# The last half-step of a two-layer decoder trunk: a different inverse root, store queue, place of the norm's weights and number of idle matmuls

## The chip, the cores and the metric

The kernel runs on one core of one Trainium2 chip. The metric is the device time of one execution in microseconds; times given for a kernel are medians over several runs. A profile is one execution taken with the hardware profiler. Its span goes from the first to the last instruction of the program.

The engines are called PE or TensorE (matmul), DVE or VectorE, ACT or ScalarE, POOL or GpSimd, and SP or SyncE (here only issuing DMA transfers). ACT, too, issues some of the transfers, in order with its arithmetic.

## What is computed

The input is 512 tokens of 1024 values. One layer with a convolution module and one with stick-breaking attention each hold two half-step feed-forward blocks. The change lies in the last of the four blocks and in the norm that ends the computation:

```
def rms_norm(x, g):
    xf = x.astype(jnp.float32)
    y = xf * lax.rsqrt(jnp.mean(xf * xf, axis=-1, keepdims=True) + RMS_EPS)
    return (y * g.astype(jnp.float32)).astype(x.dtype)

def swiglu_ffn(x, w_gate, w_up, w_down):
    return (jax.nn.silu(x @ w_gate) * (x @ w_up)) @ w_down

    # at the end of reference(), for the last layer:
    h = h + HALF_STEP * swiglu_ffn(rms_norm(h, ffn2_norm[layer]), ...)
    return rms_norm(h, final_norm)
```

## The kernel before

**Layout.** All is kept transposed: eight chunks of 128 channels (`d` = 0 to 7) on the partitions, 512 tokens along the free dimension. `res[d]` holds the running sum, in the tile `xpar`, which holds the input and the parameters too. Each fp32 product is made of three matmuls of high and low parts (`mm3`, lines 365 to 367). The channel of a norm's weight is a partition, so the weight is a per-partition scale (`col("final", d)`); the inverse root differs by token, so it has to be laid out as a row that is equal on all partitions.

**Order of the work.** The feed-forward blocks are planned: `planned` (line 461) adds steps with estimated costs, and `Plan.issue` writes them out in an order found from these costs. Only the last part, `tail` (line 1479), is written out by hand for PE, VectorE, ScalarE and GpSimd: the lines 1571 to 1611 are the order on each of these four engines. SP is not among them. The plan covers the output chunks 0 to 4 of the last third; `tail` takes the chunks 5, 6 and 7 (`a`, `b`, `e`) and works on two halves of 256 tokens (`h` = 0 and 1), so that the first half's norm and stores run while the second half's products are made.

**The parts of `tail`.** `product(d, h)` makes the matmuls into `pe`. `leave(d, h)` adds half of that to `res` on VectorE (line 1496) and squares the sum on ScalarE (line 1500). `add` (line 1503) adds the squares up in `acc_out`. `sums(h)` sums over the partitions: eight small matmuls against a column of 1/1024 (line 397), the last four from the squares of chunk 7 directly. The result `ss` has the 256 tokens as 128 partitions by 2.

`root(h)` makes the inverse root of these 2 columns. `inv_root` (lines 403 to 410) takes a first guess from the bits of the number and does three Newton steps of three instructions each; with the addition of epsilon (line 1520) these are 12 dependent instructions on VectorE. The result is split in a high and a low part (lines 1523 and 1524).

`diagonal_rows(h)` multiplies the identity by these columns, one block on VectorE (line 1535) and one on ScalarE (line 1533) for each part, and `row(h)` (line 1542) multiplies a matrix of ones by them, which gives the row of factors on all partitions, twice: `pb_out..v` for VectorE, and `pb_out..a`, which `rows(h)` copies to SBUF for GpSimd (line 1561).

The output of a chunk is made in one of two ways. Either `gain(d, h)` has multiplied by the weight on ScalarE earlier (line 1546), and `scale(d, h)` multiplies by the row on GpSimd (line 1551); that is so for the chunks 5, 6, 7 of the first half and 5, 6 of the second. Or `scale` does both at once on VectorE (line 1554). It then issues the store of 128 KB at once (line 1557): on SP for odd chunks, on ScalarE's queue for even ones. A store on ScalarE's queue waits there, in order, until its data is made.

`idle()` (line 1567) issues 16 matmuls whose result nobody reads, between the last sums and the last row. `STEADY` is their number.

## Time and profile before

| | us |
|---|---|
| median of 3 runs | 1886.19 |
| lowest and highest of them | 1885.01, 1886.81 |
| the profiled execution's own time | 1885.87 |
| its span | 1884.1 |
| PE busy | 1863.1 (99% of the span) |
| VectorE busy | 1495.5 (79%) |
| ScalarE busy | 996.1 (53%) |
| GpSimd busy | 219.4 (12%) |

Busy PE time counts matmuls that overlap in the pipeline, so 99% does not say that PE works at its peak. Times in the timeline count from the start of the span. In the chain of waits, each piece is the work or wait that the next piece was released by, followed back from the last instruction. In the rows of a timeline stand the start, the length, the engine, the line, the operation, output and inputs, and, in brackets, how long the engine had been idle before and what ended that. The queue of an engine that issues a DMA is written with a q (ACTq, SPq).

### The profile page before, as it was taken

The numbers are of one execution on the slowest core, as the hardware profiler recorded it, in microseconds if no ns is written. First come the engines' busy times: TensorE is split into PE (matmuls) and PEld (weight loads), VectorE is DVE, ScalarE is ACT, GpSimd is POOL, SyncE is SP. The second block draws the span as 40 slices with busy tenths as digits, with TensorE's granted clock in tenths as the row PEclk, the third lists the DMA queues.
The fourth block names the chain that finished last, engine by engine and source line by source line (L and its number), as shares of the span: only waits on it lengthen the run. The fifth ranks groups of instructions, "written<-read, shape, count | busy, mean of one in ns | idle before, by whom it ended". The sixth has DMA issues, their size and how long they took to land.

```text
span 1884.1 us, 29763 instructions
## 1 busy us (share of the span) xinstructions
PE 1863.1 (99%) x11558; PEld 1676.5 (89%) x11560; DVE 1495.5 (79%) x2494; ACT 996.1 (53%) x1670; POOL 219.4 (12%) x240
## 2 busy tenths in 40 slices
PE   9999999999999999999999999999999999999998
PEld 7889989878998999898898999988888779899897
DVE  8968868689789669677995976978999689678595
ACT  5535535696655446345452544646777655345253
POOL 0000000079700000000000000004454100000000
PEclk9999999999999999999999999999999999999999
DMA  5565666644413322323252332352322132323232
GB/s 183 173 218 202 246 211 232 239 147 172 140 57 101 112 90 90 134 69 122 84 173 79 112 113 90 125 163 83 90 76 88 51 104 87 130 73 124 79 111 78
DMA packets 74269, 238.04 MB, mean 126 GB/s; under 512 B 8464, under 2 KB 11152, under 8 KB 74128
## 3 DMA queue, kind: packets, MB, share of 16 engines
q1 hardware_dynamic: 65776, 209.41, 33.6%
q10 hardware_dynamic: 8352, 26.74, 3.7%
q8 instruction: 90, 1.47, 0.3%
q14 instruction: 51, 0.42, 0.1%
HBM read 200.46 MB, written 31.46 MB: 123 GB/s over the span
## 4 chain that ended last, share of the span: by engine, by line
PE 87%; DVE 6%; DMA 3%; ACT 2%; issue 1%; POOL 0%; DVEq 0%; ACTq 0%; SPq 0%; POOLq 0%
PE bank L365 12%; PE bank L366 12%; PE bank L367 12%; PE bank L661 11%; PE bank L663 11%; PE bank L662 11%; DMA raw<-in_gu_dram 2%; PE z L1383 2%; DVE pc L1071 1%; PE pa L365 1%; PE pa L366 1%; PE pa L367 1%; PE po L367 1%; PE po L365 1%; PE po L366 1%
## 5 line engine op out<-in xcount | busy, mean ns | idle before, releaser
L459 ACT CAST high<-raw 128x1024 fp32r<-128x1024 f32 (+1 forms) x199 | 202.6, 1018 | 277.0 <-PE bank L366 220.1
L366 PE MATMUL bank<-hlo,high 128*128 128x512 f32 x686 | 267.0, 389 | 0.0
L365 PE MATMUL bank<-hhi,high 128*128 128x512 f32 x686 | 267.0, 389 | 0.0
L367 PE MATMUL bank<-hhi,low 128*128 128x512 f32 x686 | 266.9, 389 | 0.0
L460 DVE TENSOR_TENSOR low<-raw,high 128x1024 fp32r<-128x1024 f32 (+1 forms) x199 | 234.3, 1178 | 16.1 <-ACT high L459 15.7
L781 DVE SCALAR_TENSOR_TENSOR xpar<-bank,xpar 128x512 f32<-128x512 f32 x93 | 64.2, 691 | 153.3 <-PE bank L367 153.0
L661 PE MATMUL bank<-thi,wh 128*128 128x256 f32 x544 | 154.6, 284 | 1.0 <-ACT u L707 0.6
L661 PE MATMUL bank<-thi,sh 128*128 128x256 f32 x544 | 154.2, 283 | 0.3 <-ACT bank L699 0.3
L662 PE MATMUL bank<-xlo_f,high 128*128 128x256 f32 x544 | 153.9, 283 | 0.0
L663 PE MATMUL bank<-xhi_f,low 128*128 128x256 f32 x544 | 153.9, 283 | 0.0
L662 PE MATMUL bank<-tlo,sh 128*128 128x256 f32 x544 | 153.9, 283 | 0.0
L663 PE MATMUL bank<-thi,sl 128*128 128x256 f32 x544 | 153.9, 283 | 0.0
L663 PE MATMUL bank<-thi,wl 128*128 128x256 f32 x544 | 153.9, 283 | 0.0
L662 PE MATMUL bank<-tlo,wh 128*128 128x256 f32 x544 | 153.9, 283 | 0.0
L661 PE MATMUL bank<-xhi_f,high 128*128 128x256 f32 x544 | 153.9, 283 | 0.0
L367 PEld LDWEIGHTS bank<-hhi,low 128*128 128x128 f32 x686 | 128.8, 188 | 26.9
L365 PEld LDWEIGHTS bank<-hhi,high 128*128 128x128 f32 x686 | 128.8, 188 | 26.3
L366 PEld LDWEIGHTS bank<-hlo,high 128*128 128x128 f32 x686 | 128.8, 188 | 26.0
L365 PE MATMUL bank<-xhi_f,high 128*128 128x512 f32 x320 | 126.2, 394 | 0.6 <-ACT high L258 0.6
L367 PE MATMUL bank<-xhi_f,low 128*128 128x512 f32 x320 | 125.4, 392 | 0.0
L366 PE MATMUL bank<-xlo_f,high 128*128 128x512 f32 x320 | 125.4, 392 | 0.0
L460 DVE TENSOR_TENSOR sl<-st,sh 128x1024 fp32r<-128x1024 f32 x68 | 82.9, 1219 | 41.1 <-ACT sh L459 41.1
(362 smaller groups left out, 5296.4 us busy)
## 6 DMA issues: line engine op xcount, KB each, us to landing
raw<-in_gu_dram SPq DMA_DIRECT2D x174, 512.0 KB, 3.4
raw<-in_dna_dram SPq DMA_DIRECT2D x64, 512.0 KB, 3.5
plo<-in_pw_dram SPq DMA_DIRECT2D x24, 512.0 KB, 4.2
aparth<-phi ACTq DMA_DIRECT2D x24, 512.0 KB, 3.6
apartl<-plo ACTq DMA_DIRECT2D x24, 512.0 KB, 3.9
raw<-in_dnb_dram SPq DMA_DIRECT2D x32, 384.0 KB, 3.3
high<-aparth SPq DMA_DIRECT2D x21, 512.0 KB, 3.3
low<-apartl SPq DMA_DIRECT2D x21, 512.0 KB, 4.2
```

Of the source, the lines that this page charges most:

```text
L365: PE.matmul(ps, w[0], x[0], start=first, stop=False)
L366: PE.matmul(ps, w[0], x[1], start=False, stop=False)
L367: PE.matmul(ps, w[1], x[0], start=False, stop=last)
L459: plan.add("A", a, lambda: A.copy(sub(hi()), sub(src())), r=[src], w=[hi], rank=rank)
L460: plan.add("V", v, lambda: V.tensor_sub(sub(lo()), sub(src()), sub(hi()).bitcast(F32)), r=[src, hi], w=[lo], rank=rank)
L661: PE.matmul(d, a[0], b[0], start=start and q == 0, stop=False, skip_group_check=True)
L662: PE.matmul(d, a[0], b[1], start=False, stop=False, skip_group_check=True)
L663: PE.matmul(d, a[1], b[0], start=False, stop=last_, skip_group_check=True)
L781: add("V", 0.62, lambda d=d, pd=pd: V.scalar_tensor_tensor(res[d], pd(), 0.5, res[d], op0=ALU.mult, op1=ALU.add), r=[pd], w=[("res", d)], ...
L1071: add("V", 0.66 * f + 0.06 * half, lambda x=x, q=q: V.scalar_tensor_tensor(pc(), x(), q, pc(), op0=ALU.mult, op1=ALU.add), r=[gl], w=[pc], ...
L1383: PE.matmul(dst, st, m[:, a:b], start=False, stop=True, skip_group_check=True)
```

## The change

Four things are changed, all in `tail`:

- `root` takes a square root on ScalarE (with epsilon as its bias, from a new tile), then on VectorE the reciprocal and one Newton step; the table that the square root needs is loaded on ScalarE by an instruction of its own behind the first square of `tail`.
- The first half's stores are all issued on SP; the second half's stay on SP and ScalarE by turns.
- Of the second half, the chunks 0 to 4 too get the norm's weight on ScalarE. These five are placed ahead of the first half's diagonals, and those of the chunks 5 and 6, which stood behind the second root, now stand behind `rows(0)`. VectorE then only multiplies by the row for the chunks 0 to 4; chunk 7 of the second half is done as before. A new argument of `scale` says which chunks go to GpSimd; they are the same as before.
- `STEADY` is 8 instead of 16.

```
-STEADY = 16
+STEADY = 8
...
         def root(h):
             y, v = (fp.tile([P, 2], F32, name=f"{x}_out{h}") for x in ("y", "v"))
-            V.tensor_scalar_add(v, ss[h], RMS_EPS)
-            inv_root(y, v, f"out{h}", fp)
+            t = fp.tile([P, 2], F32, name=f"t_out{h}")
+            A.activation(y, ss[h], AF.Sqrt, bias=eps)
+            V.tensor_scalar(v, ss[h], -0.5, -0.5 * RMS_EPS, op0=ALU.mult, op1=ALU.add)
+            V.reciprocal(y, y)
+            V.tensor_mul(t, y, y)
+            V.tensor_mul(t, v, t)
+            V.scalar_tensor_tensor(y, t, 1.5, y, op0=ALU.add, op1=ALU.mult)
...
-        def scale(d, h):
+        def scale(d, h, on_pool=False):
             sl = TOKENS[h]
             if (d, h) in o:
-                G.tensor_mul(o[d, h], o[d, h], rs[h])
+                if on_pool:
+                    G.tensor_mul(o[d, h], o[d, h], rs[h])
+                else:
+                    V.tensor_mul(o[d, h], o[d, h], pb[h, "v"])
...
-            (nc.sync if d % 2 else nc.scalar).dma_start(out[:, d, sl], o[d, h])
+            (nc.sync if d % 2 or h == 0 else nc.scalar).dma_start(out[:, d, sl], o[d, h])
...
+        eps = fp.tile([P, 1], F32, name="eps_out")
         a, b, e = ds
...
+            V.memset(eps, RMS_EPS)
             product(a, 0)
             leave(a, 0)
+            A.preload_act_table_set("sqrt_and_others")
             add(a, 0)
...
             for d in (5, 6, 7):
                 gain(d, 0)
+            for d in range(5):
+                gain(d, 1)
             diagonal_rows(0)
...
             rows(0)
+            for d in (5, 6):
+                gain(d, 1)
             for d in (0, 5):
-                scale(d, 0)
+                scale(d, 0, d > 4)
...
             root(1)
-            for d in (5, 6):
-                gain(d, 1)
             diagonal_rows(1)
             row(1)
             rows(1)
             for d in (0, 5, 1, 2, 6, 3, 4, 7):
-                scale(d, 1)
+                scale(d, 1, d in (5, 6))
```

## The prediction

> **What bounds the kernel now.** First the head of the page, for the scale, then the chain of waits over the last 12 us, since every edit lies there.

> ```profile
> span 1884.1 us, 29763 instructions
> ```
> ```profile
> 1872.25 0.42 DVE xpar L1496
> 1872.67 0.79 DVE out L1554 x2
> 1873.46 0.43 ACT sqe L1500
> ...
> 1874.57 3.50 PE pw_out L1567 x16
> ...
> 1878.35 0.48 DVE out L1554
> ```

> The chain's columns are start, length, and what ran. The last product leaves PSUM at 1872.25, its square follows at 1873.46 and the first scaled output at 1878.35. Two pieces are not what they seem. The two DVE scalings between 1872.67 and 1873.46 read nothing that the square needs, and the 3.50 us of idle matmuls stand for a wait that runs beside them on VectorE: the root. Next the ACT queue ahead of that square, and the first and last small step of the root, from the timeline:

> ```profile
> 1873.07 0.34 ACTq L1557 DMA_DIRECT2D out_dram<-out  x1
> 1873.46 0.42 ACT L1500 ACTIVATE sqe<-xpar 128x256 f32<-128x256 f32 x1 [1.92 <-DVE out L1554]
> 1873.93 0.64 PE L397 MATMUL ss_out<-onesD,sqe 128*128 128x1 f32 x4 [1.38 <-ACT sqe L1500]
> 1874.61 0.16 DVE L1520 TENSOR_SCALAR v_out<-ss_out 128x2 f32<-128x2 f32 x1 [0.77 <-PE ss_out L397]
> 1876.97 0.17 DVE L1523 CAST dp_out<-y_out 128x2 fp32r<-128x2 f32 x1
> ```
> ```profile
> 1871.62 2.10 POOL L1551 TENSOR_TENSOR out<-out,rs_out 128x256 f32<-128x256 f32 x3 [374.87 <-ACT rs_out L1561]
> ```

> The input of the square is there at 1872.67, but ACT holds a store of an earlier half that it may only issue when GpSimd's second product (1871.62 + 2 x 0.70 = 1873.02) is done: 1873.07, 0.34 long, then the square. TensorE stood idle for 1.38 us when the last sums began at 1873.93. The root lasts from 1874.61 to 1876.97: 2.36 us, 12 dependent steps of 0.197 us.

> Last, stretches of the end, with granted clock, DMA share and GB/s in the last three columns:

> ```profile
> 1874.40:1877.70 3.30, 3.30 (x17) 3.30 (x17) 2.64 (x16) 1.43 (x4) 0.00 (x0) 0.50 0.48 170
> 1877.80:1881.10 3.30, 0.75 (x6) 0.54 (x5) 2.44 (x6) 0.44 (x2) 1.41 (x2) 1.00 0.41 138
> 1878.30:1879.70 1.40, 0.25 (x3) 0.04 (x1) 1.35 (x4) 0.37 (x1) 0.67 (x1) 1.00 0.00 0
> 1879.70:1882.90 3.20, 0.00 (x0) 0.00 (x0) 1.09 (x3) 0.00 (x0) 0.74 (x2) 0.73 0.97 328
> ```

> From 1879.70 on the DMA engines are full (0.97) for 3.2 us: the eight stores of 128 KB of the second half. So the end follows the first of those stores, and what comes behind it is hidden by the transfers. The clock was 0.50 under the idle matmuls and 1.00 afterwards, when the rows of factors were made.

> **The change, part by part.** I shift the old times step by step.

> *Table load.* The trace has one of the same kind, and the ACT gap into which this one goes:

> ```profile
> 1537.39 1.28 ACT L675 ACT_TABLE_LOAD   x1
> ```
> ```profile
> 1862.72 0.42 ACT L1500 ACTIVATE sqe<-xpar 128x256 f32<-128x256 f32 x1 [1.74 <-DVE xpar L1496]
> ```

> 1.28 us go into 1.74 us of idle time: nothing. Without that cover the square of the first half would be late, and with it an addition that the sums need only some 3 us later. The one constant written to a column at the start lies in an idle VectorE: nothing.

> *ScalarE's queue in the first half.* It gets a square root that waits for the sums, and behind it eight multiplications by the norm's weights (three old, five new), all ahead of the diagonals.

> ```profile
> L1500 ACT ACTIVATE sqe<-xpar 128x256 f32<-128x256 f32 x6 | 2.4, 419 | 6.8 <-DVE xpar L1496 4.9 <-DVE out L1554 1.9
> L1546 ACT ACTIVATE out<-xpar 128x256 f32<-128x256 f32 x5 | 2.2, 495 | 0.6 <-DVE out L1554 0.6
> L1533 ACT ACTIVATE dg_out<-ident,dp_out 128x128 fp32r<-128x128 f32 x4 | 1.4, 394 | 4.5 <-DVE dp_out L1523 4.5
> L572 ACT ACTIVATE acc_out<-xpar 128x512 f32<-128x512 f32 x1 | 0.6, 632 | 0.1
> ```
> ```profile
> 1865.20 1.29 ACT L1546 ACTIVATE out<-xpar 128x256 f32<-128x256 f32 x3
> 1869.21 0.70 ACT L1533 ACTIVATE dg_out<-ident,dp_out 128x128 fp32r<-128x128 f32 x2 [2.72 <-DVE dp_out L1523]
> 1870.13 0.76 ACT L1500 ACTIVATE sqe<-xpar 128x256 f32<-128x256 f32 x2 [0.23 <-DVE xpar L1496]
> ```
> ```profile
> 1866.65 0.16 DVE L1520 TENSOR_SCALAR v_out<-ss_out 128x2 f32<-128x2 f32 x1 [1.80 <-PE ss_out L397]
> ```

> The square root on 2 elements is not in the trace. 419 and 632 ns at 256 and 512 elements give 0.83 ns per element and 0.21 us fixed; a per-partition operand adds 495 - 419 = 76 ns. Estimate 0.28 us; bounds 0.21 (the fixed part) and 0.39 (the nearest real row, the diagonals). It runs from 1866.65 to 1866.93, the eight multiplications start at 1866.83 and follow by (1.29 - 0.49) / 2 = 0.40 us, so the diagonals start at 1870.03 rather than 1869.21 and end at 1870.73. The shorter root brings nothing in this half: ACT is late now. Who waits:

> ```profile
> 1870.51 0.40 PE L1542 MATMUL pb_out0v<-dg_out,onesr 128*128 128x256 f32 x2
> 1870.97 0.28 PE L365 MATMUL pe<-hhi,high 128*128 128x256 f32 x1
> ```
> ```profile
> 1870.59 0.43 DVE L1503 TENSOR_TENSOR acc_out<-acc_out,sqe 128x256 f32<-128x256 f32 x1 [0.15 <-ACT sqe L1500]
> 1870.94 0.48 DVE L1554 SCALAR_TENSOR_TENSOR out<-xpar,pb_out0v 128x256 f32<-128x256 f32 x1
> 1871.34 0.42 DVE L1503 TENSOR_TENSOR acc_out<-acc_out,sqe 128x256 f32<-128x256 f32 x1
> 1871.67 0.47 DVE L1554 SCALAR_TENSOR_TENSOR out<-xpar,pb_out0v 128x256 f32<-128x256 f32 x1
> ```

> TensorE's second factor matmul (1870.63) waits for the second diagonal until 1870.77, and the rest of the last product stands behind it: ready at 1872.39 instead of 1872.25. On VectorE it is more. The squares start at 1870.65, not 1870.13, so the addition starts at 1871.11 instead of 1870.59, and then come, by the row starts above, 0.35, 0.40, 0.33 and 0.40 us of addition and scaling until the last product may leave PSUM: 1872.59. VectorE decides: **+0.34 us**. At best nothing is lost.

> *Stores of the first half on SP alone.* ACT no longer stands behind GpSimd. The square starts at 1872.59 + 0.42 + 0.04 = 1873.05 instead of 1873.46; the two multiplications of the second half that are now issued before it (copy of the row at about 1871.3, then 0.3 and 2 x 0.40) end before that. Net so far **-0.41 us**. SP takes four issues more:

> ```profile
> L1557 SPq DMA_DIRECT2D out_dram<-out x8: 332/338/425, 1872.4 to 1880.8; - x8
> ```

> Eight at 0.34 to 0.43 us from 1871.9 on end by 1875.4, in an order that also waits on GpSimd (to 1873.8). The first store of the second half comes to SP after 1877: about 2 us of cover. Without it, each issue would cost its 0.4 us at the end.

> *The root of the second half.* Old: 12 steps, 2.36 us. New: the square root (0.28), 0.04 to VectorE, then reciprocal, two products and one fused step at 0.197 = 0.79; the scaled copy of the sums runs beside the square root. 1.11 us, so **-1.25**. A reciprocal is in no row; I give it the step of the other 128x2 rows, at most twice that. The fp32r cast then starts at 1875.31 instead of 1876.97: -1.66.

> *Eight idle matmuls and the rows.*

> ```profile
> 1874.43 3.63 PE L1567 MATMUL pw_out<-dg_out,onesr 128*128 128x256 f32 x16
> 1874.79 0.41 PE L1567 MATMUL pw_out<-dg_out,onesr 128*128 128x256 f32 x1
> 1877.90 0.41 PE L1542 MATMUL pb_out1v<-dg_out,onesr 128*128 128x256 f32 x2
> 1878.15 0.40 PE L1542 MATMUL pb_out1a<-dg_out,onesr 128*128 128x256 f32 x2
> ```
> ```profile
> 1877.48 0.39 ACT L1533 ACTIVATE dg_out<-ident,dp_out 128x128 fp32r<-128x128 f32 x1
> ```
> ```profile
> 1878.59 0.37 ACT L1561 COPY rs_out<-pb_out1a 128x256 f32<-128x256 f32 x1 [0.72 <-PE pb_out1a L1542]
> 1878.86 0.34 ACTq L1557 DMA_DIRECT2D out_dram<-out  x1
> ```

> The last diagonal is ready at 1877.87 - 1.66 = 1876.21, and the second row matmul starts at 1876.25 (old 1878.02: 0.11 us were lost behind the sixteenth idle matmul). The idle ones start 0.41 earlier, at 1874.02; eight at the old pace (0.36 for the first, then (3.50 - 0.36) / 15 = 0.21 each) end by 1875.87, so they hold nobody up. But they no longer last the 3.4 us after which the clock came back in the windows above. If the clock is still 0.50, the two row matmuls behind start 0.21 apart and the last takes 0.41, as an idle one did, instead of 0.40 - 0.12 = 0.28: the row for the copy is ready at 1876.25 + 0.42 + 0.41 = 1877.08 instead of 1878.55. The copy stands ahead of the first store on ACT (1878.59, then 1878.86), so that store moves by **-1.47 us**. At full clock it is 1876.25 + 0.24 + 0.28 = 1876.77, or -1.78.

> The window in which the clock was halved held a PE gap of only 1.38 us and the small sums; now both shrink, but a second gap follows the eighth idle matmul. Half clock is likelier: of the 3.4 us before the rows, from 1872.7 on, eight idle matmuls fill only 1.8 us at half clock and some 1 us at full, and the rest is small sums or nothing. [...]

> *The second half's scaling.* Five three-operand steps (0.48) become plain products (0.42) and run behind the first store, hidden by the transfers; the first one ends ahead of the copy's 0.27 us. Nothing.

> **Sum.** +0.34 - 0.75 - 1.25 + 0.19 (half clock, less the 0.11) = -1.47: span 1884.1 to 1882.6, the profiled run 1885.87 to 1884.4. The three runs' median is 0.3 us above that run: **1884.7 us**.

> **Rivals.**
> (a) The clock is full at the row: -1.78, 1884.4 us. For it: the gap shrinks from 1.38 to about 0.8 us, and the idle time comes in two pieces. Against it: the 0.50 that followed 1.38 us. [...]
> (b) Slower than before: the square is not in the square root's table set, and the sets change at each turn. On the path lie one load before the squares of the second half's products (1.28 + 0.03) and the rest of one before the second square root, 0.57 us of which the sums do not cover: -1.47 + 1.31 + 0.57 = +0.41, 1886.6 us. It decides once loads on the path exceed 1.47 us. Against it: squares (L572, L1500) run behind the load at 1537.39, made for the silu, with none of their own. [...]
> (c) ACT is not late: the scheduling of its eight multiplications costs less than the estimate and the last product leaves at 1872.25 as before. 0.34 more: -1.81, 1884.4 us with half clock.
> (d) SP's eight issues take longer than 0.65 us each, run out of their cover, and push the second half's stores back by three issues of 0.4: -1.47 + 1.2, 1885.9 us. Against it: no issue in the row above took over 0.43 us.

> **How the numbers follow.** Forecast 0.52, (a) 0.28, (b) 0.06, (c) 0.07, (d) 0.07. Faster or slower means by over 0.2%, 3.8 us, about what a measurement of this kernel can tell from no change. No case reaches that: the whole stretch behind the last product is 12 us, 3.2 of them full transfers. 0.03 on each side are left for what I have not seen. Range: from (a) and (c) together (1884.1) less 0.7 for the spread of the runs (1885.01 to 1886.81), 1883.4, to the forecast with the dear square root and reciprocal (+0.3) and the same spread, rounded up to take in (d): 1886.0.

> **What would show it.** In the profile after: one table load near 1861; the last square 0.04 us behind its input; the leave of the last product at about 1872.6 with VectorE, not TensorE, in front of it; the cast 1.1 us behind the sums; the clock at 0.50 under the last row matmuls; transfers of 3.2 us from about 1878.3. A second load, a gap in the transfers, or a square that still waits on a queue would prove me wrong.

## The result

Over 22 runs each, the changed kernel takes 1882.89 us (median) and the kernel before 1885.56 us; the ratio is 0.9986, with a 95% interval of 0.9979 to 0.9992. That is 2.6 us less, with an interval of 1.5 to 4.0 us. The time lies within 0.2% of the one before, to which I gave a chance of 0.94, but outside my range, and the gain is larger than the 1.5 us of the forecast.

The profiled execution has a span of 1879.1 us, 5.0 us less than before. Only part of that is the change. The first small sum of the first half marks the start of the tail's second half; ahead of it TensorE has the same instructions in the same order. First the timeline row of the kernel before, then that of the changed one:

```profile
1865.66 0.50 PE L397 MATMUL ss_out<-onesD,acc_out 128*128 128x1 f32 x4
```
```profile
1862.48 0.50 PE L397 MATMUL ss_out<-onesD,acc_out 128*128 128x1 f32 x4
```

3.18 us of the difference are there already when that sum starts. From it to the end of the span ("the tail", below) it is 1884.1 - 1865.66 = 18.4 us before and 1879.1 - 1862.48 = 16.6 us after: 1.8 us. To compare a step, add 3.18 to its time after.

The changed kernel's chain of waits, over its end:

```profile
1869.40 0.35 DVE xpar L1496
1869.77 0.43 ACT sqe L1500
1870.24 0.62 PE ss_out L397 x4
1870.88 0.27 ACT y_out L1521
1871.17 0.16 DVE v_out L1522
1871.44 0.17 DVE t_out L1524
1871.64 0.17 DVE t_out L1525
1871.83 0.17 DVE y_out L1526
1872.03 0.18 DVE dp_out L1528
1872.23 0.41 ACT dg_out L1538
1872.74 0.64 PE pb_out1v L1547 x2
1873.40 0.42 DVE out L1559
```

The two scalings of VectorE and the idle matmuls are gone from the chain. The square follows its input, and the root stands in the chain itself, with the square root on ScalarE at its head. ScalarE's timeline shows the first half's queue, with its one table load in the gap foreseen and the eight multiplications ahead of the diagonals:

```profile
1857.82 1.28 ACT L1583 ACT_TABLE_LOAD   x1
1859.54 0.42 ACT L1500 ACTIVATE sqe<-xpar 128x256 f32<-128x256 f32 x1 [0.44 <-DVE xpar L1496]
...
1863.47 0.26 ACT L1521 ACTIVATE y_out<-ss_out,eps_out 128x2 f32<-128x2 f32 x1 [1.35 <-PE ss_out L397]
1863.63 3.30 ACT L1551 ACTIVATE out<-xpar 128x256 f32<-128x256 f32 x8
1866.83 0.69 ACT L1538 ACTIVATE dg_out<-ident,dp_out 128x128 fp32r<-128x128 f32 x2
```

TensorE's timeline and the stretches behind the last sums (granted clock, DMA share and GB/s in the last three columns):

```profile
1870.24 0.61 PE L397 MATMUL ss_out<-onesD,sqe 128*128 128x1 f32 x4 [0.57 <-ACT sqe L1500]
1870.70 1.19 PE L1575 MATMUL pw_out<-dg_out,onesr 128*128 128x256 f32 x8
1872.74 0.63 PE L1547 MATMUL pb_out1v<-dg_out,onesr 128*128 128x256 f32 x2 [0.84 <-ACT dg_out L1538]
```
```profile
1870.70:1871.90 1.20, 1.19 (x10) 0.99 (x9) 0.83 (x6) 0.26 (x1) 0.27 (x1) 1.00 0.79 266
1872.70:1873.60 0.90, 0.86 (x4) 0.60 (x4) 0.28 (x2) 0.23 (x1) 0.00 (x0) 1.00 0.77 258
1874.80:1878.00 3.20, 0.00 (x0) 0.00 (x0) 0.74 (x3) 0.00 (x0) 0.70 (x2) 0.57 0.92 321
```

The reader is to see three things. The idle time ahead of the last sums fell from 1.38 to 0.57 us. Eight idle matmuls took 1.19 us at full clock (1.00 in 1870.70 to 1871.90), and the last rows had it too (1.00 in 1872.70 to 1873.60). And the transfers still fill the end (0.92 over 3.2 us, where it was 0.97).

### The profile page after: what moved, and what is told of

The parts are those of the page before. It is cut to its first block, busy times and chain, and to the rows that moved or that the text cites. A ratio compares the mean times of both kernels' runs of the same rounds, so it can differ in the third digit from the quotient of the medians.

```text
span 1879.1 us, 29747 instructions
## 1 busy us (share of the span) xinstructions
PE 1859.1 (99%) x11552; PEld 1672.5 (89%) x11552; DVE 1491.9 (79%) x2481; ACT 999.3 (53%) x1678; POOL 220.0 (12%) x240
## 3 DMA queue, kind: packets, MB, share of 16 engines
q8 instruction: 90, 1.47, 0.3%
## 4 chain that ended last, share of the span: by engine, by line
PE 90%; DVE 5%; ACT 2%; DMA 2%; issue 1%; POOL 0%; DVEq 0%; ACTq 0%; SPq 0%
PE bank L365 12%; PE bank L367 12%; PE bank L366 12%; PE bank L661 11%; PE bank L663 11%; PE bank L662 11%; PE z L1383 2%; DVE pc L1071 1%; DMA raw<-in_gu_dram 1%; PE pa L365 1%; PE pa L367 1%; PE pa L366 1%; PE po L367 1%; PE po L365 1%; PE po L366 1%
## 5 line engine op out<-in xcount | busy, mean ns | idle before, releaser
L365 PE MATMUL bank<-hhi,high 128*128 128x512 f32 x686 | 267.0, 389 | 0.0
L365 PEld LDWEIGHTS bank<-hhi,high 128*128 128x128 f32 x686 | 128.8, 188 | 26.2
L365 PE MATMUL bank<-xhi_f,high 128*128 128x512 f32 x320 | 125.3, 392 | 1.2 <-ACT high L258 1.2
```

The source lines that it names most:

```text
L365: PE.matmul(ps, w[0], x[0], start=first, stop=False)
```

## The experiments

Theory A: the change is worth what its tail is shorter by, and the rest of any one difference is spread ahead of the tail. Theory B: it brings 2.7 us, in tails that the one profile before does not show. Beside that stands the question that the prediction lost: what sets the clock at the last rows.

The tail and the clock at the last row matmuls of each profiled execution (tail: span less start of the first small sum), and the timed ratio to the kernel before:

| | tail starts | tail | clock at the rows | ratio, 95% interval |
|---|---|---|---|---|
| before | 1865.66 | 18.4 | 1.00 | |
| after | 1862.48 | 16.6 | 1.00 | 0.9986 (0.9979 to 0.9992) |
| e1_null | 1865.27 | 18.6 | 0.50 | 1.0 (0.9991 to 1.0009) |
| e11_null2 | 1865.48 | 18.6 | 0.50 | 1.0 (0.9992 to 1.0009) |
| e2_again | 1862.58 | 16.6 | 1.00 | 0.9988 (0.9979 to 0.9997) |
| e9_again2 | 1862.98 | 16.6 | 1.00 | 0.9988 (0.9979 to 0.9997) |
| e3_root8 | 1865.07 | 17.6 | 0.50 | 0.9994 (0.9985 to 1.0003) |
| e4_stores | 1864.23 | 17.7 | 1.00 | 0.9993 (0.9984 to 1.0001) |
| e5_steady16 | 1866.19 | 16.6 | 1.00 | 0.9987 (0.9977 to 0.9996) |
| e6_steady0 | 1865.50 | 16.9 | 0.50 | 0.9991 (0.9982 to 1.0001) |
| e7_nogains | 1866.94 | 16.7 | 0.50 | 0.9991 (0.9982 to 1.0001) |
| e8_lategains | 1864.27 | 16.4 | 1.00 | 0.9991 (0.9982 to 1.0) |
| e10_late2 | 1863.68 | 16.4 | 1.00 | 0.9986 (0.9977 to 0.9995) |

**e1_null and e11_null2.** No edit.

> The kernel before, unchanged. Theory A (the change is worth 1.5 to 1.8 us, all in the tail, and the rest of the measured 2.7 us is spread from run to run ahead of the tail): no change in time (within 1 us), a tail of 18.5 us from the first small sum of the first half to the end of the span, as in the profile before, and a start of that tail anywhere between 1861 and 1867 us. Theory B (the change really brings 2.7 us, because the tail before is usually longer than in its one profile): a tail of over 19 us.

> The kernel before once more. Theory A: no change; a tail between 18.4 and 18.7 us. Theory B: a tail over 19 us at a phase of the clock's window not seen yet.

No change in time (1885.15 us beside 1884.92, 1884.63 beside 1884.34), tails of 18.6 us. None of this kernel's three profiled tails is over 19 us, so nothing supports the reason that theory B gave. The 0.2 us above the first profile come from the clock, which is still 0.50 when the row begins (0.50 in 1874.60 to 1877.90):

```profile
1877.25 0.82 PE L1542 MATMUL pb_out1v<-dg_out,onesr 128*128 128x256 f32 x2
```

0.82 us for the two, where the first profile has 0.41. The median of the kernel before was 1886.19, 1885.56, 1884.92, 1885.09 and 1884.34 us in series of 3, 22, 33, 31 and 27 runs (the second contains the first).

**e2_again and e9_again2.** No edit to the changed kernel.

> The kernel after, unchanged, measured anew. Theory A: -1.5 to -2.0 us, a tail of 16.6 us at full clock at the last rows, 16.9 at half clock. Theory B: -2.7 us again, and a tail under 16 us or a head that starts its tail 1 us earlier than the null run does.

> The changed kernel once more, since its timed gains so far (2.7 and 1.9 us, 2.4 us over all runs) lie above the 1.85 to 2.0 us that its tail is shorter by. Theory A (only the tail counts): a tail of 16.6 or 16.9 us and -1.9 us. Theory B (some 0.5 us lie ahead of the tail or in tails before that no profile has caught): -2.4 us or more again.

1883.04 beside 1884.92 us and 1882.05 beside 1884.34 us: -1.9 and -2.3 us. The tail is 16.6 us each time, with the clock at 1.00 at the rows. All runs together (44 of the changed kernel; 134 of the one before, with one of over 6000 us left out) have medians of 1882.64 and 1884.98 us; the means differ by 2.4 us, with a 95% interval of 2.0 to 2.8. The tail accounts for 1.8 to 2.0 us of it.

**e3_root8.** Only the root, its table load and eight idle matmuls, on the kernel before:

```
-STEADY = 16
+STEADY = 8
-            V.tensor_scalar_add(v, ss[h], RMS_EPS)
-            inv_root(y, v, f"out{h}", fp)
+            A.activation(y, ss[h], AF.Sqrt, bias=eps)
...
+            A.preload_act_table_set("sqrt_and_others")
```

> Only the new root (with its table load) and 8 idle matmuls; stores and weights as before. Theory A: the root saves 1.2 us and the idle queue 0.1, so -1.3 us at full clock and -1.0 at half clock, with the last square still behind the GpSimd store. If the root's gain were taken back by the idle queue or by ScalarE: under 0.5 us.

The tail is 17.6 us, 0.8 to 1.0 below the kernel before; timed, 1883.44 beside 1884.92 us, an interval that includes no change. The square still waits behind the GpSimd store, TensorE idles as long as before, and the clock falls to 0.50:

```profile
1873.34 0.73 PE L397 MATMUL ss_out<-onesD,sqe 128*128 128x1 f32 x4 [1.39 <-ACT sqe L1500]
1873.93 2.06 PE L1572 MATMUL pw_out<-dg_out,onesr 128*128 128x256 f32 x8
1875.96 0.82 PE L1547 MATMUL pb_out1v<-dg_out,onesr 128*128 128x256 f32 x2
1876.59 0.63 PE L1547 MATMUL pb_out1a<-dg_out,onesr 128*128 128x256 f32 x2
```
```profile
1873.80:1877.20 3.40, 3.40 (x14) 2.88 (x13) 1.81 (x10) 1.75 (x5) 0.00 (x0) 0.50 0.44 150
```

At half clock the rows last 1.26 us here (1875.96 to 1877.22), at full clock 0.86 us in the changed kernel (1872.74 to 1873.60). Alone, then, the root gives some 0.4 us of its gain back at the rows, where the forecast had 0.3 for half clock. What the forecast missed is that with the stores moved as well the clock stayed full (1.00 in the changed kernel's three executions).

**e4_stores.** Only the queue of the first half's stores, on the kernel before:

```
-            (nc.sync if d % 2 else nc.scalar).dma_start(out[:, d, sl], o[d, h])
+            (nc.sync if d % 2 or h == 0 else nc.scalar).dma_start(out[:, d, sl], o[d, h])
```

> Only the first half's stores moved to SP. Theory A: the last square starts 0.04 us behind its input, and all behind it moves with it: -0.75 us. If the sixteen idle matmuls, which are paced by the clock's window, hold the row: 0 to -0.3 us.

Tail 17.7 us, 0.7 to 0.9 less; 1883.65 beside 1884.92 us. Sixteen idle matmuls take 2.13 us, at a clock of 1.00, where they took 3.63 us in the first profile (0.50 in 1874.40 to 1877.70); the row then waits for the diagonals and not for them:

```profile
1871.74 0.60 PE L397 MATMUL ss_out<-onesD,sqe 128*128 128x1 f32 x4 [0.62 <-ACT sqe L1500]
1872.21 2.13 PE L1567 MATMUL pw_out<-dg_out,onesr 128*128 128x256 f32 x16
1875.45 0.63 PE L1542 MATMUL pb_out1v<-dg_out,onesr 128*128 128x256 f32 x2 [1.12 <-ACT dg_out L1533]
```
```profile
1872.00:1876.50 4.50, 3.20 (x24) 2.73 (x23) 3.43 (x19) 1.33 (x5) 0.30 (x1) 1.00 0.56 190
```

So the move of the stores brings the shorter wait, and in this execution full clock behind it (1.00).

**e5_steady16 and e6_steady0.** The changed kernel with 16 idle matmuls and with none:

```
-STEADY = 8
+STEADY = 16
```
```
-            idle()
```

> The changed kernel with 16 idle matmuls instead of 8. Idle queue not binding (clock full behind the last sums, 16 x 0.12 = 1.9 us, over before the diagonals are ready 2.2 us after the queue's start): tail 16.6 us as with 8. Idle queue binding (clock halved there, 3.4 us): the rows wait, tail 17.6 us or more.

> The changed kernel without any idle matmul. If they keep the clock up at the last rows: the clock falls to 0.50 ahead of the rows, which take 0.3 us more, tail 16.9 us. If the short gap ahead of the last sums is what keeps it up: tail 16.6 us or, by the first sums of the chain being unaffected, nothing changes at all.

Sixteen: tail 16.6 us, as with eight. At full clock they hold nobody up: the rows start 10.26 us behind the first sum (1876.45 - 1866.19), as with eight (1872.74 - 1862.48). So halving the number gained nothing in this execution. None: tail 16.9 us, the rows at half clock (0.50 in 1874.30 to 1877.10):

```profile
1873.26 0.61 PE L397 MATMUL ss_out<-onesD,sqe 128*128 128x1 f32 x4 [0.57 <-ACT sqe L1500]
1875.76 0.82 PE L1547 MATMUL pb_out1v<-dg_out,onesr 128*128 128x256 f32 x2 [1.89 <-ACT dg_out L1538]
1876.38 0.63 PE L1547 MATMUL pb_out1a<-dg_out,onesr 128*128 128x256 f32 x2
```

The first wait is 0.57 us as in the changed kernel; what is new is 1.89 us of idleness behind it. In this execution the clock fell before the rows without the idle matmuls, which in the changed kernel take up part of that time.

**e7_nogains and e8_lategains (repeated as e10_late2).** The first takes the five multiplications out; the second moves two of them:

```
-            for d in range(5):
-                gain(d, 1)
```
```
-            for d in range(5):
+            for d in range(3):
                 gain(d, 1)
...
             root(1)
+            for d in (3, 4):
+                gain(d, 1)
```

> The changed kernel without the five new multiplications by the weights ahead of the first half's diagonals; VectorE scales and weighs these chunks at once, as before. Theory A: ScalarE is no longer late, the last product leaves PSUM 0.25 us earlier (6.6 us behind the first small sum, not 6.84), VectorE's slower steps hide behind the stores: tail 16.4 us. Rival (the weights on ScalarE shorten the end): first store 0.06 us later, tail 16.7 us.

> The changed kernel with two of the five multiplications (chunks 3 and 4) moved behind the second square root, where ScalarE waits 1.1 us for the root. Theory A: the last product leaves at 6.6 us, tail 16.4 us, so 0.2 us below the changed kernel. Rival: ScalarE still too late for the first half's diagonals, no change: 16.6 us.

> The version with two multiplications moved behind the second root, once more. Theory A: a tail of 16.4 us (16.7 at half clock), -2.1 us against the kernel before and 0.2 below the changed kernel. Theory B: as much faster than the changed kernel's repeat as nothing, with a tail of 16.6 us.

In both, the last product leaves 0.27 us earlier relative to the first sum: 1873.51 - 1866.94 = 6.57 us and 1870.84 - 1864.27 = 6.57 us, against 1869.32 - 1862.48 = 6.84 us in the changed kernel. The last-product rows on VectorE, of the first, the second and the changed kernel:

```profile
1873.51 0.42 DVE L1496 SCALAR_TENSOR_TENSOR xpar<-pe,xpar 128x256 f32<-128x256 f32 x1
```
```profile
1870.84 0.42 DVE L1496 SCALAR_TENSOR_TENSOR xpar<-pe,xpar 128x256 f32<-128x256 f32 x1
```
```profile
1869.32 0.41 DVE L1496 SCALAR_TENSOR_TENSOR xpar<-pe,xpar 128x256 f32<-128x256 f32 x1
```

With two multiplications moved, the tail is 16.4 us in both executions, 0.2 below the changed kernel, as expected. Without the five it is 16.7: the rows ran at half clock there, so this run does not tell what the five are worth at the end. Timed, 1883.55 us beside 1885.09 and 1882.01 beside 1884.34: the version with two moved is 1.5 and 2.3 us below the kernel before (the first interval reaches up to no change), and its 0.2 us over the changed kernel are too few for the timed runs to show.

The first two, e7 and e8, show something else about the clock. Up to the rows TensorE does the same work in both, with the same idle times, and one has half and the other full clock:

```profile
1876.94 0.82 PE L1547 MATMUL pb_out1v<-dg_out,onesr 128*128 128x256 f32 x2 [0.85 <-ACT dg_out L1538]
```
```profile
1874.27 0.63 PE L1547 MATMUL pb_out1v<-dg_out,onesr 128*128 128x256 f32 x2 [0.85 <-ACT dg_out L1538]
```

0.82 us in the first, 0.63 in the second, each behind 0.85 us of idle time. So TensorE's work up to the rows did not by itself decide it here.

```profile
1872.96:1876.37 3.41, 2.51 (x21) 2.22 (x19) 2.91 (x12) 1.34 (x4) 2.03 (x3) 1.00 0.59 201
1876.37:1879.79 3.42, 1.25 (x4) 0.98 (x4) 2.58 (x10) 1.06 (x3) 1.12 (x2) 0.50 0.49 166
```
```profile
1870.20:1873.61 3.41, 2.60 (x22) 2.31 (x20) 2.91 (x12) 2.23 (x6) 2.11 (x3) 1.00 0.57 194
1873.61:1877.02 3.41, 0.86 (x4) 0.61 (x4) 2.76 (x10) 1.06 (x3) 1.40 (x2) 1.00 0.55 190
```

Against the first sum, e8's stretch began 0.09 us earlier (1870.20 - 1864.27 = 5.93 us, 1872.96 - 1866.94 = 6.02), and so one product matmul more begins in it: eleven matmuls of 256 columns, against ten in e7. This count sorts all 13 tails: behind a stretch at full clock in which 8 to 10 of these matmuls begin (before, e1, e11, e3, e6, e7) the clock fell to 0.50, behind 11 to 19 (the seven others) it stayed at 1.00. (In the first profile of the kernel before it was back when the rows began, after a stretch of 3.41 us at half clock that sixteen of these matmuls filled.) That is a count of these tails and not a test of the cause, and it does not carry over to other matmuls: ahead of the tail, where most have 512 columns, the count of columns does not sort the stretches cleanly.

By this count one can estimate how often the changed kernel loses its clock at the rows. If the last of these times lies less than 0.6 us ahead of the rows, fewer than eleven such matmuls begin in the stretch before it (from the starts in the trace of the changed kernel); that is 0.6 of 3.41 us, about one execution in six, if all positions are equally likely. With sixteen idle matmuls (e5) it is never fewer than thirteen. So the halved number gained nothing that the runs show, and by this estimate it costs some 0.3 us (16.9 against 16.6 us of tail, e6) in one execution of six.

## Why the prediction was wrong

*Table load, constant, SP's issues, order of the chain.* Right. The load took 1.28 us in its gap and no second one followed, so rival (b) falls; SP's issues took 0.33 to 0.45 us each, and behind the eighth (1872.51) SP had no more to issue before the second half's first store (1874.18), so rival (d) falls.

*ScalarE late in the first half, +0.34.* Right in mechanism, nearly in size: the diagonals start at 1866.83 + 3.18 = 1870.01 (forecast 1870.03), the last product leaves at 1872.50 (forecast 1872.59), +0.25. The runs with the multiplications removed or moved take 0.27 us back.

*The square, -0.41 net.* 1869.77 + 3.18 = 1872.95 instead of 1873.46: -0.51, the difference being mostly the 0.09 above.

*The root, -1.25.* From the square root (1870.88) to the cast (1872.03) it is 1.15 us where the old one took 2.36: -1.21. The square root took 0.26 us (forecast 0.28), the reciprocal one step. One statement was wrong: the scaled copy of the sums did not run beside the square root but waited for it:

```profile
1871.17 0.16 DVE L1522 TENSOR_SCALAR v_out<-ss_out 128x2 f32<-128x2 f32 x1 [0.27 <-ACT y_out L1521]
1871.25 0.16 DVE L1523 RECIPROCAL y_out<-y_out 128x2 f32<-128x2 f32 x1
```

That puts 0.08 us ahead of the reciprocal.

*Half clock at the rows, +0.30.* This is the step that failed. I took the 0.50 that followed 1.38 us of idle time, counted how little of the last 3.4 us up to the rows was full-rate work, and judged half clock likelier. That those 3.4 us decide the clock was my estimate, which no run shows. In all three executions of the changed kernel the rows ran at 1.00. Rival (a), which I had priced at -1.78 and given 0.28, is what happened: ScalarE's first store of the second half is issued at 1873.86 + 3.18 = 1877.04 us instead of 1878.86, -1.82, and the tail is 1.8 to 2.0 us shorter. By the count above, what was wrong is the stretch that I counted. In the 13 executions the clock changed only at times whole multiples of 3.41 us apart, and of all stretches of 3.41 us ahead of the rows the one that ends just as they begin holds the fewest matmuls, eight. The stretches that were over last before the rows in the three executions ended 0.9 to 1.6 us earlier and held 13 to 15, more than the 8 to 10 behind which the clock fell in other tails. The 1.38 us of idle time, too, lay in a stretch with full clock (1.00 in 1871.00 to 1874.30); the 0.50 came behind it. I had seen that the wait shrinks and given too little to it. In one execution each, stores alone kept full clock, the root alone did not, and without idle matmuls it was lost again.

*The base and its spread.* The half clock is not the largest part of the miss. The median of three runs, 1886.19, lay above every longer series of the same kernel (1884.34 to 1885.56), and I allowed 0.7 us for the spread, although the three runs themselves reached 1.2 us below their median (1885.01). Even with the forecast gain of 1.5 us, the base of 1885.56 would have given 1884.1. With 2.0 us it gives 1883.6, still in the range; the measured 1882.89 is below it. Of the 1.8 us between forecast and time, the base is 0.6, the clock 0.3 to 0.5, and the rest, 0.7 to 0.9, lies outside what the tails show.

*What stays open.* The timed gain over all runs, 2.4 us (2.0 to 2.8), is at or above the 1.8 to 2.0 us of the tails. The tail started at 1862.5 to 1863.0 us in three executions of the changed kernel and at 1865.3 to 1865.7 in three of the kernel before, but at 1863.7 to 1866.9 in seven of kernels that share this code up to the tail, one of which has only more idle matmuls at its end. Part of this spread goes with the clock. The time ahead of the tail without full clock (from the start to the first grant of it, at 4.0 to 10.7 us, and later stretches at 0.50) was 11.0 to 11.6 us in the first three, 14.8 to 17.7 in the second three, and 10.9 to 17.4 in the seven. Over the 13 the tail starts some 0.4 us later for each such us (correlation 0.75). So the two groups of three probably owe much of their difference to where the clock's changes fell. Whether the last 0.4 us of the timed gain are a difference ahead of the tail or chance, the runs do not settle.

## What to carry to other kernels

Look for instructions in an in-order queue that wait for another engine, and ask what useful work stands behind them: one store that ScalarE held for GpSimd cost 0.7 to 0.9 us of tail (e4), and behind the idle time that it made on TensorE (1.38 us, 0.62 in e4) the clock fell to 0.50 as well. When a change moves the wait ahead of a burst of matmuls, cost the clock by the new wait, not by the profile's old one, and keep both values in the range: with the same waits of 0.62 and 0.85 us the same row matmuls ran at 0.50 in e7 and at 1.00 in e8. In these 13 tails the count of matmuls in the last stretch of 3.41 us that was over before the burst told the two apart (8 to 10 against 11 to 19); that it does so in another kernel is not shown. Where a kernel of 1.9 ms is to be judged by 2 us, read the gain from the stretch that was changed, and take the base from a long series.

## What the runs showed of the hardware beyond that

The same TensorE instructions ahead of the tail took from 1862.48 to 1866.94 us in 13 profiled executions: 4.5 us, about twice what the change is worth. At 1.00 a pair of row matmuls took 0.63 us (e8), at 0.50 it took 0.82 us (e7), each behind 0.85 us of idle time.
